# A decoder block on one core: the attention's projections, turns and softmaxes in another order, the rotation on another engine

## The chip, the cores and the metric

The kernel runs on one core of a Trainium2 chip. A core has a tensor engine (PE; its weight loads are listed apart as PEld), a vector engine (DVE), a scalar engine (ACT), GpSimd (POOL) and a queue that only issues transfers (SP). PE writes its products to eight banks of PSUM; the other data lies in SBUF. The metric is the time of one execution in microseconds. Three runs of the kernel before gave 361.92, 362.18 and 362.21, median 362.18. One execution was profiled; its trace is what the numbers below come from.

## The reference

One decoder layer on 256 tokens of width 1024. Two attention branches of eight heads with 64 columns each run side by side: MoBA, whose q and k are normalized and rotated (with 256 tokens it is plain causal attention), and FoX, whose scores get a bias from a cumulated forget gate. Two sigmoid gates merge them, and a gated feed-forward part follows.

```python
h = rms_norm(x, attn_norm_g)
proj = h @ w_in
qa, ka, va, qb, kb, vb, f_logit, g_logit = split(proj)
qa = partial_rope(rms_norm(split_heads(qa)), pos)      # the first 16 columns of each head
ka = partial_rope(rms_norm(split_heads(ka)), pos)
o_a = merge_heads(moba_attention(qa, ka, va))
qb, kb = rms_norm(split_heads(qb)), rms_norm(split_heads(kb))
o_b = merge_heads(forgetting_attention(qb, kb, vb, log_sigmoid(f_logit + b_forget)))
gates = sigmoid(g_logit + b_gate)
x = x + (gates[0] * (o_a @ w_branch_moba) + gates[1] * (o_b @ w_branch_fox)) @ w_out
up = rms_norm(x, ffn_norm_g) @ w_ffn_up
u, g = split(up)
x = x + (silu(causal_depthwise_conv(g)) * u) @ w_ffn_down
```

## The kernel before

**Products.** Every matrix product is made of three: each float32 operand is split into a high part (ACT copies it, `whi`, line 136) and the rest (DVE subtracts, `wlo`, line 137), and PE adds high x high, high x low and low x high. A weight comes by a transfer of 1 MB into `raw` (three buffers), and is split in two units of 1024 columns; `whi` and `wlo` have six buffers each, and `use` asks for units five ahead. A unit's split can only start when PE has read the buffer that it gets. These 120 pairs of splits run through the whole program beside whatever else DVE and ACT do.

**Stages.** `project_qk` computes q and k of MoBA from the first loads (banks `pq`, `pk`). `project` computes one of the other q, k, v in 48 products of 512 columns (line 291), `twin` one 256-column pair of a weight in 48 products of 256 columns (lines 513 to 515); `gate(c)` is such a pair for both merge gates, read out of its bank by DVE (line 522). `finish_qk` normalizes q or k per head: ACT squares the bank (305), DVE sums (306), a chain of small operations gives the factor (219 to 223, 309), DVE multiplies the bank by it (315), and for MoBA rotates 16 columns of each head (322 to 325). `turn_qk` transposes the result on PE (341, 64 columns each) and ACT copies it to `qT`, `kT` (346). `scores` multiplies q and k (434) into six banks; `softmax` adds mask or bias (450), takes exponentials on ACT (453) and scales (458), a pair of heads at a time. `turn` transposes the probabilities (469, 48 transposes in six banks, copied out by ACT at 473), `values` multiplies them with v (485), and ACT and DVE split the result into `oh`, `ol` (499, 500). The forget gate is a small product (362), summed by another (372), then a chain on a few rows (378 to 399) that ends with a transfer through DRAM and `forget_bias` (408 to 414).

**Order.** PE runs in the order in which the code is written. For DVE, ACT and POOL a scheduler sets the order at build time by priority; `soon()` raises what is inside it by 45 places of the program. Each engine then runs its list strictly in order. A bank is handed on when its last reader is done, so a product that starts a bank can wait for DVE or ACT.

The code at the end (lines 536 to 594) writes the attention as: MoBA's q, k; v; FoX's q; forget gate; turn of MoBA's q, k; FoX's k with the scores of MoBA in its middle; FoX's v; gate 0; turn of FoX's q, k and of MoBA's probabilities; gate 1; MoBA's values and FoX's scores; gates 2 to 6; turn of FoX's probabilities; gate 7; FoX's values. Behind that come the branch projection, the output projection and the feed-forward part, which the change leaves alone.

Of the kernel before, what the change touches and what calls it, by code (L numbers as in the profile page):

```python
# [32 lines left out]
SOON = 45  # L33
# [11 lines left out]
def decoder_block(ctx, tc, a, out):  # L45
# [36 lines left out]
    chunks = [("qkv", m, h) for m in range(4) for h in range(2)]  # L82
    chunks += [("wg", c) for c in range(KT)]
# [18 lines left out]
    def load(upto):  # L102
        while state["next"] <= min(upto, len(units) - 1):
# [30 lines left out]
            for j in range(n):  # L134
                s = slice(j * w, (j + 1) * w)
                i = nc.scalar.activation(hi[:, s], raw[:, s], AF.Copy)  # L136
                d = nc.vector.tensor_tensor(lo[:, s], raw[:, s], hi[:, s].bitcast(F32), op=ALU.subtract)  # L137
                if (c, h) == (("qkv", 0, 1), 0):
                    after(i, rs_done[0])
                    after(d, rs_done[1])  # L140
                if (c, h) == (("qkv", 0, 0), 0):
                    first_lo.append(d)
                if c[0] == "head" and j == 0:
                    after(d, xlo)
# [91 lines left out]
    def norm1_sums():  # L236
        nc.scalar.activation(flat[:, 0], xss[:, 1], AF.Copy)
        low = nc.gpsimd.tensor_tensor(flat[:, 1], xss[:, 1], flat[:, 0].bitcast(F32), op=ALU.subtract)
        for i in casts:
            after(i, low)  # L240
        ssp = bank()[:, 0:S]
# [56 lines left out]

    def finish_qk(br, pts):
# [11 lines left out]
        for m, (isk, pt) in enumerate(pts):  # L311
            qn = T([P, NT, NH, HD], "qn", 2)
            qns.append(qn)
            for t in range(NT):
                nc.vector.tensor_tensor(qn[:, t], pt[t].rearrange("p (h d) -> p h d", h=NH),
                                        f[:, m, t, :, None].to_broadcast([P, NH, HD]), op=ALU.mult)
            if br == 0:
                rc, rsn = rope[isk]
                p1 = T([P, NT, NH, 16], "p1", 1)
                p2 = T([P, NT, NH, 16], "p2", 1)  # L320
                x16 = qn[:, :, :, 0:16]
                nc.vector.tensor_tensor(p1, x16, rc[:, :, None, :].to_broadcast([P, NT, NH, 16]), op=ALU.mult)
                nc.vector.tensor_tensor(p2, x16, rsn[:, :, None, :].to_broadcast([P, NT, NH, 16]), op=ALU.mult)
                nc.vector.tensor_tensor(qn[:, :, :, 0:8], p1[:, :, :, 0:8], p2[:, :, :, 8:16], op=ALU.add)
                nc.vector.tensor_tensor(qn[:, :, :, 8:16], p1[:, :, :, 8:16], p2[:, :, :, 0:8], op=ALU.add)
# [3 lines left out]
    qT = T16(4, "qT", F32)  # L329
    kT = T16(4, "kT", F32)  # L330
    halves = (slice(0, HD), slice(HD, P))

    def turn_qk(qn, br, isk):
# [8 lines left out]
        dst = (kT if isk else qT).rearrange("p b (m c) -> p m b c", m=4)  # L342
# [23 lines left out]
    def row(i):  # L366
        return gates[:NH, i // 2, i % 2]
# [49 lines left out]
    oh = T16(KT, "oh")  # L417
    ol = T16(KT, "ol")
    probs = {}
    last_exp = []  # L420

    def scores(br):
# [5 lines left out]
        for n, pair in enumerate(range(4)):  # L428
            for t in range(NT):
                for c, q in enumerate(QUARTERS[t]):  # L430
                    seen = slice(0, (q + 1) * HD) if t == 0 else slice((3 - q) * HD, S)
                    keys = slice(seen.start + (1 - t) * P, seen.stop + (1 - t) * P)
                    for j, r in enumerate(halves):
                        nc.tensor.matmul(piece(n, t, j)[halves[c], seen], qT[r, pair, q * HD:(q + 1) * HD], kT[r, pair, keys], start=True, stop=True)  # L434
# [7 lines left out]
    def softmax(br, pair, sps):  # L442
        s = T([P, 2, 384], "s", 4)
        nm = T([P, 2, 2], "nm", 4)
        l = T([P, 2, 2], "l", 4)
        for j in range(2):
            h = 2 * pair + j
            sp = sps[j]
            for i, c in enumerate((slice(0, 128), slice(128, 384))):
                nc.vector.tensor_tensor_reduce(s[:, j, c], sp[i], mask3[:, c] if br == 0 else bias[:, h, c],  # L450
                                               scale=1.0, scalar=3e38, op0=ALU.add, op1=ALU.min, accum_out=nm[:, j, i:i + 1])
            for i, c in enumerate((slice(0, 128), slice(128, 384))):
# [9 lines left out]
    def turn(br):  # L462
        pT = T([P, 4, 2, 384], "pT")
# [7 lines left out]
        for i in range(3):  # L471
            for h in range(2):
                nc.scalar.activation(dst[:, h, 8 * i:8 * i + 8], tps[i][h].rearrange("p (g c) -> p g c", g=8), AF.Copy)
        for pair in range(4):
            probs[br, pair] = pT[:, pair]

    def values(br):
        ops = banks()
        o4 = [o.rearrange("p (h b t) -> p h b t", h=2, b=4) for o in ops]

        def product(o, r, k, b, c, pair, j, start, stop):
# [6 lines left out]
        for i, k, b, c in ((0, 0, 0, two), (1, 0, 2, both), (1, 1, 1, two)):  # L488
            for pair in range(4):
                for j, m in enumerate(halves):  # L490
                    product(o4[i][m, c, pair], full, k, b, c, pair, j, b != 1 and pair == 0, False)
        for pair in range(4):
            for j, m in enumerate(halves):
                product(o4[0][m, 0, pair], halves[0], 0, 0, one, pair, j, False, pair == 3)
                product(o4[1][m, 0, pair], halves[1], 1, 1, one, pair, j, False, pair == 3)
        b = slice(4 * br, 4 * br + 4)
        for i in range(2):
            h, l = (v[:, b, i * P:(i + 1) * P].rearrange("p b (h t) -> p h b t", h=2) for v in (oh, ol))
            copied = nc.scalar.activation(h, o4[i], AF.Copy)
            nc.vector.tensor_tensor(l, o4[i], h.bitcast(F32), op=ALU.subtract)  # L500
        return copied
# [17 lines left out]
    def gate(c):  # L519
        gp = bank()  # L520
        twin("wg", c, gp, xh, xl)
        return nc.vector.tensor_tensor(gates[:, c], gp.rearrange("p (b t) -> p b t", b=2), rsB[:, None, :].to_broadcast([P, 2, S]), op=ALU.mult)
# [7 lines left out]
    def soon():  # L530
        return tc.high_priority(offset=SOON)

# [3 lines left out]
    pq, pk, pv = banks(), banks(), banks()  # L536
# [8 lines left out]
    with soon():  # L545
        qn, kn = finish_qk(0, ((0, pq), (1, pk)))
# [3 lines left out]
    pq, pk = banks(), banks()  # L550
    project(3, pq, 0)
    project(3, pq, 1)
    with soon():
        forget_a()
    turn_qk(qn, 0, 0)
    turn_qk(kn, 0, 1)
    with soon():
        qn, = finish_qk(1, ((0, pq),))
    def between():
        with soon():  # L560
            forget_b()
    project(4, pk, 0, between)
    with soon():
        sps = scores(0)
        for pair in range(2):
            done = softmax(0, pair, sps[pair])
    forget_chain(done)
    project(4, pk, 1)
    with soon():
        kn, = finish_qk(1, ((1, pk),))  # L570
    for pair in range(2, 4):
        done = softmax(0, pair, sps[pair])
# [4 lines left out]
    first = gate(0)  # L577
    with soon():
        forget_bias(first)
    turn_qk(qn, 1, 0)  # L580
    turn_qk(kn, 1, 1)
    turn(0)
    gate(1)
    values(0)
    for pair, sp in enumerate(scores(1)):
        softmax(1, pair, sp)
    gate(2)
    gate(3)
    gate(4)
    gate(5)  # L590
    gate(6)
    turn(1)
    gate(7)
    copied = values(1)
# [206 lines left out]
```

## Time and profile before

| | us |
|---|---|
| median of three runs | 362.18 |
| profiled execution, time | 361.99 |
| its span in the trace | 360.2 |
| PE busy | 355.0 |
| DVE busy | 276.0 |
| ACT busy | 217.9 |
| POOL busy | 26.3 |

The mean granted clock of PE was 0.999. The attention that the change touches lies between 27 and 132 us of the span. Rows of the trace give a start, a duration, the engine, the line, the operation and what is written from what; rows of groups give the busy time and the mean of one in ns, then the idle time ahead of it and what ended that.

### The profile page before, as it was taken

The numbers are of one execution on the slowest core, as the hardware profiler recorded it, in microseconds if no ns is written. First come the engines' busy times: TensorE is split into PE (matmuls) and PEld (weight loads), VectorE is DVE, ScalarE is ACT, GpSimd is POOL, SyncE is SP. The second block draws the span as 40 slices with busy tenths as digits, with TensorE's granted clock in tenths as the row PEclk, the third lists the DMA queues.
The fourth block names the chain that finished last, engine by engine and source line by source line (L and its number), as shares of the span: only waits on it lengthen the run. The fifth ranks groups of instructions, "written<-read, shape, count | busy, mean of one in ns | idle before, by whom it ended". The sixth has DMA issues, their size and how long they took to land.

```text
span 360.2 us, 7565 instructions
## 1 busy us (share of the span) xinstructions
PE 355.0 (99%) x3119; PEld 337.2 (94%) x3119; DVE 276.0 (77%) x491; ACT 217.9 (60%) x363; POOL 26.3 (7%) x43
## 2 busy tenths in 40 slices
PE   9999999999999999999999999999999999999995
PEld 4788878899999999999999999999999999999994
DVE  5899698999897547875979776868677777768643
ACT  5859666988598765545876654655554554555420
POOL 2542002200000000000530000000000000000000
PEclk9999999999999999999999999999999999999999
DMA  7986665174606644455364565464565464563003
GB/s 275 402 318 244 238 229 186 56 285 186 235 3 250 231 172 152 152 216 212 140 235 173 179 235 173 179 235 162 191 231 168 185 233 149 204 225 128 0 2 116
DMA packets 12130, 68.28 MB, mean 190 GB/s; under 512 B 1688, under 2 KB 2848, under 8 KB 4672
## 3 DMA queue, kind: packets, MB, share of 16 engines
q1 hardware_dynamic: 11664, 66.62, 51.1%
q0 software_dynamic: 288, 1.19, 0.9%
q8 instruction: 24, 0.39, 0.4%
q14 instruction: 10, 0.08, 0.1%
q10 hardware_dynamic: 144, 0.00, 0.0%
HBM read 66.75 MB, written 1.06 MB: 188 GB/s over the span
## 4 chain that ended last, share of the span: by engine, by line
PE 99%; DVE 0%; issue 0%
PE bank L513 15%; PE bank L515 15%; PE bank L514 15%; PE bank L291 12%; PE bank L277 6%; PE bank L715 6%; PE bank L713 6%; PE bank L714 6%; PE bank L611 2%; PE bank L637 2%; PE bank L613 2%; PE bank L612 2%; PE bank L639 2%; PE bank L638 2%; PE bank L485 1%; PE bank L434 1%
## 5 line engine op out<-in xcount | busy, mean ns | idle before, releaser
L137 DVE TENSOR_TENSOR wlo<-raw,whi 128x1024 fp32r<-128x1024 f32 x120 | 146.8, 1227 | 51.5 <-ACT whi L136 51.4
L136 ACT ACTIVATE whi<-raw 128x1024 fp32r<-128x1024 f32 x120 | 126.4, 1058 | 74.8 <-PE bank L514 44.1
L515 PE MATMUL bank<-oh,wlo 128*128 128x256 f32 x352 | 96.8, 275 | 0.0
L513 PE MATMUL bank<-oh,whi 128*128 128x256 f32 x352 | 96.8, 275 | 0.0
L514 PE MATMUL bank<-ol,whi 128*128 128x256 f32 x352 | 96.8, 275 | 0.0
L513 PEld LDWEIGHTS bank<-oh,whi 128*128 128x128 f32 x352 | 66.1, 188 | 0.0
L514 PEld LDWEIGHTS bank<-ol,whi 128*128 128x128 f32 x352 | 66.1, 188 | 0.0
L515 PEld LDWEIGHTS bank<-oh,wlo 128*128 128x128 f32 x352 | 66.1, 188 | 0.0
L513 PE MATMUL bank<-xh,whi 128*128 128x256 f32 x128 | 35.6, 278 | 0.0
L515 PE MATMUL bank<-xh,wlo 128*128 128x256 f32 x128 | 35.3, 275 | 0.0
L514 PE MATMUL bank<-xl,whi 128*128 128x256 f32 x128 | 35.2, 275 | 0.0
L513 PEld LDWEIGHTS bank<-xh,whi 128*128 128x128 f32 x128 | 24.0, 188 | 0.5 <-DVE ol L500 0.3
L514 PEld LDWEIGHTS bank<-xl,whi 128*128 128x128 f32 x128 | 24.0, 188 | 0.0
L515 PEld LDWEIGHTS bank<-xh,wlo 128*128 128x128 f32 x128 | 24.0, 188 | 0.0
L291 PE MATMUL bank<-whi,xh 128*128 128x512 f32 x64 | 21.2, 392 | 0.0
L291 PE MATMUL bank<-whi,xl 128*128 128x512 f32 x64 | 21.0, 389 | 0.0
L291 PE MATMUL bank<-wlo,xh 128*128 128x512 f32 x64 | 21.0, 388 | 0.0
L680 DVE TENSOR_TENSOR sq<-bank,rs 128x512 f32<-128x512 f32 x22 | 15.1, 691 | 6.6 <-PE bank L515 6.5
L611 PE MATMUL bank<-oh,whi 128*128 128x256 f32 x64 | 17.7, 277 | 0.0
L613 PE MATMUL bank<-oh,wlo 128*128 128x256 f32 x64 | 17.6, 275 | 0.0
L612 PE MATMUL bank<-ol,whi 128*128 128x256 f32 x64 | 17.6, 275 | 0.0
L637 PE MATMUL bank<-xh,whi 128*128 128x256 f32 x64 | 17.6, 275 | 0.0
(179 smaller groups left out, 743.1 us busy)
## 6 DMA issues: line engine op xcount, KB each, us to landing
raw<-in_wu SPq DMA_DIRECT2D x22, 1024.0 KB, 4.8
raw<-in_wd SPq DMA_DIRECT2D x11, 1024.0 KB, 4.8
raw<-in_qkv SPq DMA_DIRECT2D x8, 1024.0 KB, 5.2
raw<-in_wg SPq DMA_DIRECT2D x8, 1024.0 KB, 5.0
raw<-in_wb SPq DMA_DIRECT2D x4, 1024.0 KB, 4.8
raw<-in_wo SPq DMA_DIRECT2D x4, 1024.0 KB, 4.8
raw<-in_head SPq DMA_DIRECT2D x6, 512.0 KB, 6.6
gates<-cd POOLq DMA_DIRECT2D x1, 1024.0 KB, 5.0
```

Of the source, the lines that this page charges most:

```text
L136: i = nc.scalar.activation(hi[:, s], raw[:, s], AF.Copy)
L137: d = nc.vector.tensor_tensor(lo[:, s], raw[:, s], hi[:, s].bitcast(F32), op=ALU.subtract)
L277: nc.tensor.matmul(pt[t], lhs[:, k, t * P:(t + 1) * P], rhs, start=(k == 0 and i == 0), stop=(k == KT - 1 and i == 2))
L291: nc.tensor.matmul(pt[t], lhs[:, k, t * P:(t + 1) * P], rhs[:, c], start=(k == 0 and i == 0), stop=(k == KT - 1 and i == 2))
L513: nc.tensor.matmul(o, wh[:, w], mh[:, k], start=(k == 0 and i == 0), stop=False)
L514: nc.tensor.matmul(o, wh[:, w], ml[:, k], start=False, stop=False)
L515: nc.tensor.matmul(o, wl[:, w], mh[:, k], start=False, stop=(k == KT - 1 and i == 1))
L611: nc.tensor.matmul(o, wh[:, w], oh[:, 4 * br + k], start=(k == 0), stop=False)
L612: nc.tensor.matmul(o, wh[:, w], ol[:, 4 * br + k], start=False, stop=False)
L613: nc.tensor.matmul(o, wl[:, w], oh[:, 4 * br + k], start=False, stop=(k == 3))
L637: nc.tensor.matmul(o, wh[:, w], mh[:, k], start=(k == 0 and i == 0), stop=False)
L713: nc.tensor.matmul(o, wh[:, w], ah, start=(p == 0 and h == 0 and c == 0), stop=False)
```

## The change

- The projections stand in another order: MoBA's q, k, then FoX's q, k (their normalization raised by 160 places), gate 0, then all four turns with the forget gate's product ahead of the last, gate 1, MoBA's scores, MoBA's v, gate 2, FoX's scores, FoX's v, gates 3 to 5, both turns of probabilities, gate 6, both values, gate 7. The list of loads follows.
- The rotation's four operations per tile go from DVE to GpSimd.
- Each gate's read out of its bank is raised by 160 places, and the softmaxes are ordered behind such a read.
- FoX's normalized q, k, their turned copies, its softmax and its turned probabilities live in the buffers of `ol`, `oh`, `qn` and `bias`, since both branches are now alive at once.
- The sigmoids of the gates are ordered behind the copies of FoX's turned probabilities, in place of its last exponential.
- The sum of the first normalization uses the bank of the warm-up.

```diff
-    chunks = [("qkv", m, h) for m in range(4) for h in range(2)]
-    chunks += [("wg", c) for c in range(KT)]
+    chunks = []
+    for m in (1, 2, "wg0", "wg1", 0, "wg2", 3, "wg3", "wg4", "wg5", "wg6", "wg7"):
+        chunks += [("wg", int(m[2:]))] if isinstance(m, str) else [("qkv", m, h) for h in range(2)]
...
+            if br == 0:
+                qn = T([P, NT, NH, HD], "qn", 2)
+            else:
+                qn = qn1[:, 4 * isk:4 * isk + 4].rearrange(...)
...
-                nc.vector.tensor_tensor(p1, x16, rc[:, :, None, :].to_broadcast([P, NT, NH, 16]), op=ALU.mult)
+                nc.gpsimd.tensor_tensor(p1, x16, rc[:, :, None, :].to_broadcast([P, NT, NH, 16]), op=ALU.mult)
...
-    def values(br):
-        ops = banks()
+    def values():
+        oh, ol = T16(KT, "oh"), T16(KT, "ol")
+        ops = [banks() for br in range(2)]
...
     def gate(c, between=None):
...
+        with soon(FIRST):
+            return nc.vector.tensor_tensor(gates[:, c], gp.rearrange("p (b t) -> p b t", b=2), rsB[:, None, :].to_broadcast([P, 2, S]), op=ALU.mult)
...
+    for isk in range(2):
+        pt = banks()
+        project(3 + isk, pt, 0)
+        project(3 + isk, pt, 1)
+        with soon(FIRST):
+            qkn += finish_qk(1, ((isk, pt),))
+    gate(0)
+    with soon():
+        for i, qn in enumerate(qkn):
+            if i == 3:
+                forget_a()
+            turn_qk(qn, i // 2, i % 2)
...
+    read = gate(1, between)
+    with soon():
+        for pair, sp in enumerate(scores(0)):
+            scaled = softmax(0, pair, sp, read)
...
+    read = gate(2)
+    with soon():
+        forget_bias(read)
+    with soon():
+        for pair, sp in enumerate(scores(1)):
+            softmax(1, pair, sp, read)
...
+    with soon():
+        turn(0)
+        last_exp[:] = [turn(1)]
     gate(6)
+    oh, ol, copied = values()
     gate(7)
```

In the changed kernel the lines are shifted: the split stands at 137 and 138, squares at 308, sums at 309, normalization at 321, transposes of q and k at 348, the forget gate's product at 369, transposes of probabilities at 483, their copies at 487, a gate's products at 531 to 533 and its read at 541.

PE, around the forget gate's product and the turns of q and k; first before (the turn of MoBA's q, k, in the middle of FoX's projections):

```order
L291 MATMUL bank<-whi,xl 128x512 x2
L291 MATMUL bank<-wlo,xh 128x512 x2
L362 MATMUL bank<-xT,wfg 32x256 x8
L341 MATMUL bank<-cst,qn 128x64 x32
L291 MATMUL bank<-whi,xh 128x512
L291 MATMUL bank<-whi,xl 128x512
L291 MATMUL bank<-wlo,xh 128x512
```

and now, between gate 0 and gate 1 (`qn` are MoBA's q and k, `ol` holds FoX's):

```order
L532 MATMUL bank<-xl,whi 128x256
L533 MATMUL bank<-xh,wlo 128x256
L348 MATMUL bank<-cst,qn 128x64 x32
L348 MATMUL bank<-cst,ol 128x64 x16
L369 MATMUL bank<-xT,wfg 32x256 x8
L348 MATMUL bank<-cst,ol 128x64 x16
L531 MATMUL bank<-xh,whi 128x256
L532 MATMUL bank<-xl,whi 128x256
```

All four turns are one piece behind gate 0; FoX's q comes third, its k last. The bank of q's second half is the one that gate 0 had, and k's tile must be normalized by DVE.

DVE, at the normalization of a FoX tile; before (FoX's q):

```order
L306 TENSOR_REDUCE ss<-sq 128x8 x2
L137 TENSOR_TENSOR wlo<-raw,whi 128x1024
L219 TENSOR_SCALAR qfv<-ss 128x16
L221 SCALAR_TENSOR_TENSOR qfv<-qfv 128x16
L222 TENSOR_TENSOR qfv<-qfv 128x16
L223 SCALAR_TENSOR_TENSOR qf<-qfv 128x16
L309 TENSOR_TENSOR qf<-qf,rsw 128x16
L315 TENSOR_TENSOR qn<-bank,qf 128x512 x2
```

and now (FoX's k, with the read of gate 0 at L541):

```order
L309 TENSOR_REDUCE ss<-sq 128x8 x2
L138 TENSOR_TENSOR wlo<-raw,whi 128x1024
L220 TENSOR_SCALAR qfv<-ss 128x16
L138 TENSOR_TENSOR wlo<-raw,whi 128x1024
L222 SCALAR_TENSOR_TENSOR qfv<-qfv 128x16
L138 TENSOR_TENSOR wlo<-raw,whi 128x1024
L223 TENSOR_TENSOR qfv<-qfv 128x16
L541 TENSOR_TENSOR gates<-bank,rsB 128x512
L224 SCALAR_TENSOR_TENSOR qf<-qfv 128x16
L138 TENSOR_TENSOR wlo<-raw,whi 128x1024
L312 TENSOR_TENSOR qf<-qf,rsw 128x16
L321 TENSOR_TENSOR ol<-bank,qf 128x512 x2
```

Four splits and the read of gate 0 stand between the sums and the normalization, where one split stood.

ACT, at the copies of the turned probabilities; before (FoX's, the second turn):

```order
L526 ACTIVATE gates<-gates,sm 128x256 x2
L136 ACTIVATE whi<-raw 128x1024 x2
L526 ACTIVATE gates<-gates,sm 128x256
L473 ACTIVATE pT<-bank 128x8x64 x6
L526 ACTIVATE gates<-gates,sm 128x256
L136 ACTIVATE whi<-raw 128x1024 x2
```

and now (`pT` MoBA's, `bias` FoX's, L545 the gates' sigmoids):

```order
L137 ACTIVATE whi<-raw 128x1024 x6
L487 ACTIVATE pT<-bank 128x8x64 x6
L487 ACTIVATE bias<-bank 128x8x64 x6
L545 ACT_TABLE_LOAD
L545 ACTIVATE gates<-gates,sm 128x256 x2
L137 ACTIVATE whi<-raw 128x1024
```

Twelve copies follow each other behind six splits; the load of the sigmoid's table, which came ahead of the second turn, is behind them.

More of the change, by code (lines that the diff above doesn't have):

```diff
@@ L366, in row @@
     def row(i):
-        return gates[:NH, i // 2, i % 2]
+        return gates[:NH, 4 + i // 2, i % 2]
     def forget_b():
@@ L440, in scores, with softmax @@
         return [[[piece(n, t, j) for t in range(NT)] for j in range(2)] for n in range(4)]
-    def softmax(br, pair, sps):
-        s = T([P, 2, 384], "s", 4)
+    def softmax(br, pair, sps, done):
+        if br == 0:
+            s = T([P, 2, 384], "s", 4)
+        else:
+            if not homes:
+                two = T([P, KT * S + 64], "ol")
+                homes.extend(two[:, i * 768:(i + 1) * 768] for i in range(2))
+                homes.extend(T([P, 1024], "qn", 2)[:, 0:768] for i in range(2))
+            s = homes[pair].rearrange("p (j c) -> p j c", j=2)
         nm = T([P, 2, 2], "nm", 4)
@@ L487, in values @@
         one, two, both, full = slice(0, 1), slice(1, 2), slice(0, 2), slice(0, P)
-        for i, k, b, c in ((0, 0, 0, two), (1, 0, 2, both), (1, 1, 1, two)):
+        for br, o4 in enumerate(o4s):
+            for i, k, b, c in ((0, 0, 0, two), (1, 0, 2, both), (1, 1, 1, two)):
+                for pair in range(4):
+                    for j, m in enumerate(halves):
+                        product(o4[i][m, c, pair], full, k, b, c, br, pair, j, b != 1 and pair == 0, False)
+        for br, o4 in enumerate(o4s):
             for pair in range(4):
                 for j, m in enumerate(halves):
[L491 to L501, printed above, removed]
+                    product(o4[0][m, 0, pair], halves[0], 0, 0, one, br, pair, j, False, pair == 3)
+                    product(o4[1][m, 0, pair], halves[1], 1, 1, one, br, pair, j, False, pair == 3)
+            b = slice(4 * br, 4 * br + 4)
+            for i in range(2):
+                h, l = (v[:, b, i * P:(i + 1) * P].rearrange("p b (h t) -> p h b t", h=2) for v in (oh, ol))
+                copied = nc.scalar.activation(h, o4[i], AF.Copy)
+                nc.vector.tensor_tensor(l, o4[i], h.bitcast(F32), op=ALU.subtract)
+        return oh, ol, copied
     def twin(kind, c, dst, mh, ml, late=False, between=None):
@@ L517, in twin, with gate @@
                     between()
[L519 removed]
+    def gate(c, between=None):
         gp = bank()
[L521 to L522 removed]
+        twin("wg", c, gp, xh, xl, between=between)
+        with soon(FIRST):
+            return nc.vector.tensor_tensor(gates[:, c], gp.rearrange("p (b t) -> p b t", b=2), rsB[:, None, :].to_broadcast([P, 2, S]), op=ALU.mult)
     def gate_sigmoid(c):
@@ L576, in decoder_block @@
     finish_v(pv, 1)
[L577 to L587, printed above, removed]
     gate(3)
```

78 lines of the change are left out of this document (32 added, 46 removed).

## The prediction

> **What bounds the kernel now.** I read the page first: its busy shares, the idle times of the tensor engine, then the chain that ended last.
>
> ```profile
> span 360.2 us, 7565 instructions
> PE 355.0 (99%) x3119; PEld 337.2 (94%) x3119; DVE 276.0 (77%) x491; ACT 217.9 (60%) x363; POOL 26.3 (7%) x43
> PEclk9999999999999999999999999999999999999999
> PE 99%; DVE 0%; issue 0%
> ```
>
> The span is a string of matrix products at full granted clock; no other engine has a share in the chain. A busy PE could still hide short waits, so I asked who PE waited for:
>
> ```profile
> PE bank L190 <- PEq L794: 0.8, 1, 0.8
> ```
>
> That is the whole answer: 0.8 us at the start, nothing later. So the change cannot take away a wait, since there is none. It can only save what PE spends on going into and out of its stretches of small products, and it can add waits. The chain, in order of time, prices the stretches (start, us, line, count):
>
> ```profile
> 27.40 21.76 PE bank L291 x96
> 49.16 1.00 PE bank L362 x16
> 50.16 1.14 PE bank L341 x32
> 51.30 2.93 PE bank L291 x12
> ...
> 54.46 2.74 PE bank L291 x12
> 57.20 2.33 PE bank L434 x46
> ...
> 76.11 0.12 PE bank L513
> ...
> 81.55 1.15 PE bank L341 x30
> 82.70 1.75 PE bank L469 x48
> 84.45 0.32 PE bank L513
> 84.76 0.12 PE bank L514
> ...
> 90.14 2.58 PE bank L485 x80
> 92.72 2.18 PE bank L434 x46
> ...
> 122.35 1.65 PE bank L469 x44
> ...
> 129.67 2.58 PE bank L485 x80
> ```
>
> A twin of 48 products takes 81.55 - 76.11 = 5.44 us (gate 0). The first product behind a stretch takes 0.32 in place of 0.12 (84.45 against 84.76), or 12 take 2.93 in place of 2.74: 0.2 us for each return.
>
> **Term 1, the stretches.** Before, small products come in six groups: forget gate and first turn, scores 0, second turn and probabilities 0, values 0 and scores 1, probabilities 1, values 1. After, five: all turns with the forget gate, scores 0, scores 1, both probabilities, both values. One return less: -0.2. The values of both branches enter their form once, not twice: some -0.1 by the same price. Scores 1 now stand alone, as scores 0 do (2.33 against 2.18 behind the values): +0.15. The forget gate lies between transposes, one more change of form: up to +0.2. Both probabilities together: some -0.15. I take -0.3, with bounds -0.6 and 0. All other products are the same ones, so nothing larger than 0.6 us can be won by this change on PE.
>
> **Term 2, the turn of FoX's k.** Here the new order puts PE right behind DVE. Times as in the trace of before as long as PE does the same: q's and k's FoX projections are 96 products of L291's kind, 27.40 to 49.16, gate 0 runs to 54.60. Then PE transposes q, k (MoBA), q (FoX), multiplies the forget gate, transposes k (FoX). Without waits that takes 1.00 + 1.14 + 1.15 + 0.2, some 3.5 us, and the last eight transposes (second half of the rows) start near 57.6. What must be ready is k's finish: two squares on ACT, then the DVE rows shown in the section on the change. Their prices stand in the groups of the trace from 20 to 136 us and in DVE's timeline:
>
> ```profile
> L305 ACT ACTIVATE sq<-bank,rsw 128x512 f32<-128x512 f32 x8 | 5.1, 676 | 0.0
> L522 DVE TENSOR_TENSOR gates<-bank,rsB 128x512 f32<-128x512 f32 x8 | 5.4, 678 | 0.9 <-PE bank L515 0.9
> ...
> 49.92 1.22 DVE L137 TENSOR_TENSOR wlo<-raw,whi 128x1024 fp32r<-128x1024 f32 x1
> 51.06 0.41 DVE L364 TENSOR_TENSOR aT<-bank,aT 128x256 fp32r<-128x256 f32 x1
> 51.39 1.27 DVE L306 TENSOR_REDUCE ss<-sq 128x8 f32<-128x512 f32 x2
> ...
> 54.62 0.17 DVE L222 TENSOR_TENSOR qfv<-qfv 128x16 f32<-128x16 f32 x1
> 55.31 1.29 DVE L315 TENSOR_TENSOR qn<-bank,qf 128x512 f32<-128x512 f32 x2
> 56.52 0.40 DVE L373 TENSOR_TENSOR gates<-bank,rsB 8x256 f32<-8x256 f32 x1
> ```
>
> A split steps on by 1.14 (51.06 - 49.92), a pair of reduces by 1.2, a pair of normalizations takes 1.29, a small operation 0.1 beside others and 0.2 in a dependent chain. ACT has one split (1.06) ahead of k's squares, whose buffer a product near 48.7 gives free; the two squares of 0.68 end at 50.4 and 51.0, the second reduce at 51.6. Behind it stand three splits and three small rows: 3 x 1.14 + 0.3, so gate 0's read starts at about 55.3, though its products end at 54.60: DVE is 0.6 to 0.7 late. That read stands ahead of k's last factors by its raised priority. From its start to the end of the second normalization: 0.6 (read, in steps) + 0.1 + 1.14 (a split) + 0.2 + 1.29 = 3.3, hence 58.6. PE, ready for it at 57.6, waits about 1.1 us in sum; the first part of it already at q's transposes, whose bank is the one that gate 0's read gives free.
>
> The rotation, now on GpSimd, runs beside this: q's MoBA tile is normalized near 47, k's near 49, and each then takes two operations of 128x256 and two of half that. By GpSimd's rows below, 0.8 us for 128x256 and 0.5 as an estimate for the half, 2.6 for a tile, k's ends at about 52, over two microseconds ahead of the first transpose at 54.6, so both are hidden; if GpSimd took twice as long on these strided shapes, k's turn would come 1 us late. DVE is rid of these eight operations, which the 55.3 above already leaves out. But GpSimd's work is not free for DVE:
>
> ```profile
> 18.87 1.76 DVE L137 TENSOR_TENSOR wlo<-raw,whi 128x1024 fp32r<-128x1024 f32 x1
> ...
> 21.50 1.21 DVE L137 TENSOR_TENSOR wlo<-raw,whi 128x1024 fp32r<-128x1024 f32 x1
> ...
> 13.80 5.74 POOL L183 TENSOR_TENSOR xss<-xss,sq 128x256 f32<-128x256 f32 x5 [4.18 <-ACT sq L179]
> 20.44 0.79 POOL L183 TENSOR_TENSOR xss<-xss,sq 128x256 f32<-128x256 f32 x1 [0.89 <-ACT sq L179]
> ```
>
> While GpSimd adds (13.80 to 19.54), a split took 1.76 us, against 1.21 at 21.50. Two splits lie beside the rotation; 0 to 2 x 0.55 = 1.1 us more. One of them has 0.4 of idle time behind it (the wait for the squares), so I take +0.35. Term 2: +1.45, bounds 0.35 (DVE in time: the 3.3 from 54.6 ends at 57.9) and 2.2.
>
> [...]
>
> **Term 3, both probabilities in one stretch.** 96 transposes need 12 banks and there are eight. So turn 1's third and fourth pair wait until ACT has copied turn 0's first ones out.
>
> ```profile
> 122.33 1.06 ACT L136 ACTIVATE whi<-raw 128x1024 fp32r<-128x1024 f32 x1 [1.67 <-PE bank L514]
> 123.30 0.49 ACT L526 ACTIVATE gates<-gates,sm 128x256 f32<-128x256 f32 x1
> 123.70 3.01 ACT L473 ACTIVATE pT<-bank 128x512 f32<-128x512 f32 x6
> ```
>
> There a split starts on ACT with the stretch (122.33, the stretch 122.35), the next operation 0.95 later, and the copies follow every 0.5 (3.01 for six). In the new order, too, a split that waits for the last product ahead of the stretch (gate 5's) stands before the copies. So copy n ends 1.1 + 0.5 n behind the stretch's start, the fourth, on which turn 1's last pair of banks depends, at 3.1. PE would be there at 1.65 + 2/3 x 1.65 = 2.75 and waits 0.35, more by a hand-over or two: 0.4. Before, the second turn had 0.1 of this kind (1.75 against 1.65 for the same transposes). Net +0.3, bounds 0 and 0.7.
>
> **What else moves, at nothing.** The MoBA softmax and its own splits run on DVE while PE computes v and gate 2 (16.3 us); FoX's bias and softmax beside v and gates 3 to 5 (27 us). DVE's busy share and the softmax's rows say that there is little room:
>
> ```profile
> 60.00:80.00 20.00, 20.00 (x107) 17.20 (x107) 19.62 (x80) 16.98 (x46) 4.38 (x9) 1.00 0.44 163
> ...
> L458 DVE TENSOR_SCALAR s<-s,r 128x256 f32<-128x256 f32 x16 | 5.4, 340 | 0.0
> L458 DVE TENSOR_SCALAR s<-s,r 128x128 f32<-128x128 f32 x16 | 4.4, 274 | 0.0
> L450 DVE CUSTOM_DVE_ANT_0 s<-bank,cst 128x256 f32<-128x256 f32 x8 | 3.2, 405 | 0.0
> L450 DVE CUSTOM_DVE_ANT_0 s<-bank,cst 128x128 f32<-128x128 f32 x8 | 2.2, 273 | 0.0
> ```
>
> (The window gives PE, PEld, DVE, ACT, POOL busy in 20 us, the clock, the DMA share.) A branch's softmax is 3.2 + 2.2 + (5.4 + 4.4)/2 = 10.3 us on DVE. Behind gate 1's read, which ends near 66, stand that, seven splits (8.0) and 2 us of small rows, so gate 2's read ends near 86.5. The bank that it frees is wanted by FoX v's second half: 66 + scores 2.5 + v 10.9 + gate 2 5.4 + scores 2.5 + six products 1.4, near 88. The cover is 1.5 to 2 us, and FoX's first scores leave their banks about as long before gate 3 wants one; beyond it a slip of DVE costs PE its own length. The sixteen sigmoids now precede the values' copies on ACT, beside gates 6 and 7; the copies still end over 1 us before the branch projection reads them. The loads come in another order, but the DMA engines are 0.44 busy in that window, and no wait of PE names one.
>
> **The sum.** The profiled execution before took 361.99 (span 360.2), 0.19 below the median of 362.18. 361.99 - 0.3 + 1.45 + 0.3 = 363.4 us.
>
> **Rivals.**
> - *DVE keeps up.* If the DVE rows up to gate 0's read are over by 54.6, only 0.35 of term 2 is left: 361.99 - 0.3 + 0.35 + 0.3 = 362.3; without term 3, 362.0. For it: DVE is rid of eight operations, and 0.6 us is within the error of such a sum of thirty rows. Against it: the late rows hang on ACT's squares, which cannot start before 49.16 and a split that ends at 49.7. It decides at a backlog of 0.6 us, some half of a split.
> - *GpSimd holds DVE longer.* Both splits are held for a whole operation, 2 x 0.79 by the row at 20.44, in place of the 0.35 in the sum: 363.4 + 1.2 = 364.6; the same if the softmax outruns its cover by 1 us. It decides where a split has no idle time behind it. Against it: no split in the trace was held for more than 0.55. [...]
> - *Faster.* The mechanism is the change of form on PE: if DVE and ACT are in time and the groups cost more than the returns show (0.6 saved), the time is 361.4. It needs both waits gone and the far bound of term 1.
> - *The change does not do what it says:* the order shows that it does; its scores stay apart in two stretches.
>
> **How the numbers follow.** Forecast (both waits, 362.9 to 364.2): 0.53. DVE keeps up (361.6 to 362.9): 0.29. Held longer (364.2 to 365.0, some beyond): 0.14. Faster: 0.04. A measurement of this kernel tells 0.2%, 0.72 us, from no change; so slower means above 362.9: 0.53 + 0.14 = 0.67; faster, below 361.45: 0.04; the rest, 0.29, is within. The range 361.7 to 365.0 leaves out the faster case and the end of the slow one.
>
> **What would show it.** PE's waits name DVE at the turns near 56 to 59 (by 1 to 2 us) and ACT at the probabilities near 116; the chain has a share of DVE; the values' 80 and both probabilities' 96 transposes appear as one piece each; a split beside the rotation lasts over 1.3 us. If PE names nobody there, terms 2 and 3 are wrong and the time is 361.7. If it names a bank at gate 3 or at v's second half, the cover that I counted was too thin.

## The result, and the profile after

| | before | after |
|---|---|---|
| median of six runs each | 362.14 | 366.14 |
| all runs | 361.92 to 362.46 | 364.58, 364.91, 365.97, 366.32, 366.58, 366.58 |
| profiled execution, its span | 361.99, 360.2 | 364.58, 362.8 |
| PE's small-product stretches, in sum | 16.38 | 19.93 |

The changed kernel is slower: the ratio is 1.0102, with a 95% interval of 1.0079 to 1.0124. Its executions fall into two groups, 364.6 to 364.9 at a mean granted clock of 0.999 to 1.0, and 366.0 to 366.6 at 0.994 to 0.995; the profiled one is the fastest. Forecast was 363.4, range 361.7 to 365.0.

The page after the change: the span, the busy times, the clock by slices, and the chain that ended last by engine.

```profile
span 362.8 us, 7564 instructions
PE 354.6 (98%) x3119; PEld 337.7 (93%) x3119; DVE 274.4 (76%) x483; ACT 218.0 (60%) x363; POOL 34.2 (9%) x51
PEclk9999999999999999999999999999999999999999
PE 94%; DVE 2%; DMA 1%; issue 1%; ACT 1%; DVEq 0%
```

DVE has lost only 1.6 us of busy time, though the rotation's 2.8 came off it; and the chain, which was 99% PE, now passes through DVE, DMA and ACT. The view of PE's waits (engine, line, waited for, us in total, times, longest) says where:

```profile
PE bank L483 <- DVE gates L541: 1.9, 1, 1.9
PE bank L191 <- PEq L812: 0.8, 1, 0.8
PE bank L348 <- DVE gates L541: 0.7, 1, 0.7
PE bank L348 <- DVE ol L321: 0.4, 1, 0.4
PE bank L278 <- ACT whi L137: 0.2, 1, 0.2
```

Two places: the turns (L348) and the probabilities (L483). PE's timeline shows both (start, us, line, count, and in brackets the idle time named):

```profile
54.17 1.21 PE L348 MATMUL bank<-cst,qn 64*128 64x64 f32 x32
55.22 0.22 PE L348 MATMUL bank<-cst,ol 64*128 64x64 f32 x1
56.17 0.71 PE L348 MATMUL bank<-cst,ol 64*128 64x64 f32 x15 [0.72 <-DVE gates L541]
...
58.29 0.97 PE L348 MATMUL bank<-cst,ol 64*128 64x64 f32 x16 [0.41 <-DVE ol L321]
59.19 0.38 PE L531 MATMUL bank<-xh,whi 128*128 128x256 f32 x1
...
113.73 1.72 PE L483 MATMUL bank<-cst,s 64*128 64x64 f32 x48
115.29 0.22 PE L483 MATMUL bank<-cst,ol 64*128 64x64 f32 x1
117.44 0.96 PE L483 MATMUL bank<-cst,ol 64*128 64x64 f32 x23 [1.92 <-DVE gates L541]
...
119.11 0.39 PE L531 MATMUL bank<-xh,whi 128*128 128x256 f32 x1
```

From its first small product to the first large one behind it the stretch of the turns takes 59.19 - 54.17 = 5.02 us, that of the probabilities 119.11 - 113.73 = 5.38. A kernel of the experiments below in which PE waits at neither place (all edits and the copies) shows what the same products take without a wait, 57.91 - 54.62 = 3.29 and 116.05 - 112.54 = 3.51:

```profile
54.62 1.21 PE L360 MATMUL bank<-cst,qn 64*128 64x64 f32 x32
...
57.91 0.39 PE L543 MATMUL bank<-xh,whi 128*128 128x256 f32 x1
...
112.54 1.72 PE L495 MATMUL bank<-cst,s 64*128 64x64 f32 x48
...
116.05 0.39 PE L543 MATMUL bank<-xh,whi 128*128 128x256 f32 x1
```

So the **turns lose 1.73, the probabilities 1.87**. Without waits the five stretches of the new order sum to 16.34 against 16.38 for the six of before, and there is one return less (0.2): -0.24. Together +3.36; the profiled executions differ by 2.59. Of the other 0.77, 0.37 lies in small gaps of PE in the first 12 us, which differ by 0.45 between two profiled executions of the changed kernel too, and 0.34 behind PE's last product; the rest is not traced.

What PE waited for is read on DVE. Its timeline at both places:

```profile
52.38 0.43 DVE L220 TENSOR_SCALAR qfv<-ss 128x16 f32<-128x16 f32 x1
52.73 1.21 DVE L138 TENSOR_TENSOR wlo<-raw,whi 128x1024 fp32r<-128x1024 f32 x1
53.86 0.42 DVE L222 SCALAR_TENSOR_TENSOR qfv<-qfv 128x16 f32<-128x16 f32 x1
54.21 1.21 DVE L138 TENSOR_TENSOR wlo<-raw,whi 128x1024 fp32r<-128x1024 f32 x1
...
55.43 0.68 DVE L541 TENSOR_TENSOR gates<-bank,rsB 128x512 f32<-128x512 f32 x1
...
57.45 1.29 DVE L321 TENSOR_TENSOR ol<-bank,qf 128x512 f32<-128x512 f32 x2
...
106.57 0.66 DVE L541 TENSOR_TENSOR gates<-bank,rsB 128x512 f32<-128x512 f32 x1
107.15 1.00 DVE L472 TENSOR_SCALAR qn<-qn,r 128x128 f32<-128x128 f32 x4
108.06 4.62 DVE L138 TENSOR_TENSOR wlo<-raw,whi 128x1024 fp32r<-128x1024 f32 x4
...
115.56 1.23 DVE L138 TENSOR_TENSOR wlo<-raw,whi 128x1024 fp32r<-128x1024 f32 x1 [1.14 <-ACT whi L137]
116.70 0.68 DVE L541 TENSOR_TENSOR gates<-bank,rsB 128x512 f32<-128x512 f32 x1
```

At the turns, gate 0's products end at 54.2, but its read starts at 55.43, behind the three splits that follow k's sums (51.24, 52.73, 54.21). At the probabilities gate 5's read starts at 116.70, three microseconds after its products, behind a split that itself waited for ACT. That split is of the first branch weight, the load that ACT waited for (timelines of SP and of ACT):

```profile
109.34 9.53 SPq L130 DMA_DIRECT2D raw<-in_wb  x4
```

```profile
114.46 2.00 ACT L137 ACTIVATE whi<-raw 128x1024 fp32r<-128x1024 f32 x2 [4.22 <-PE bank L483]
116.37 3.02 ACT L487 ACTIVATE pT<-bank 128x512 f32<-128x512 f32 x6
```

The bracket names PE for ACT's 4.22 us, but the split starts 0.38 after the load has landed (114.08). In two runs below the same load lands at 114.60 and at 113.21, and this split starts 0.38 later each time (114.98, 113.59): it is the load that it waits for. The load was issued at 109.34, when the first of the four splits at 108.06 had freed a `raw` buffer. So there were two theories to test: the wait at the turns is DVE's backlog of splits, and the wait at the probabilities is gate 5's read behind a split whose load is late. The two groups of times were a third thing to explain.

### The profile page after: what moved, and what is told of

It reads as the page before. It is cut to its first block, busy times and chain, and to the rows that moved or that the text cites. A ratio compares the mean times of both kernels' runs of the same rounds, so it can differ in the third digit from the quotient of the medians.

```text
span 362.8 us, 7564 instructions
## 1 busy us (share of the span) xinstructions
PE 354.6 (98%) x3119; PEld 337.7 (93%) x3119; DVE 274.4 (76%) x483; ACT 218.0 (60%) x363; POOL 34.2 (9%) x51
## 3 DMA queue, kind: packets, MB, share of 16 engines
HBM read 66.75 MB, written 1.06 MB: 187 GB/s over the span
## 4 chain that ended last, share of the span: by engine, by line
PE 94%; DVE 2%; DMA 1%; issue 1%; ACT 1%; DVEq 0%
PE bank L531 15%; PE bank L533 15%; PE bank L532 14%; PE bank L292 12%; PE bank L278 6%; PE bank L733 6%; PE bank L732 5%; PE bank L731 5%; PE bank L657 2%; PE bank L631 2%; PE bank L656 2%; PE bank L655 2%; PE bank L630 2%; PE bank L629 2%; PE bank L501 1%; PE bank L440 1%
```

## The experiments

Each kernel is the changed one with the edit shown, unless said otherwise; "wait" is a stretch's length beyond 3.29 (turns) or 3.51 (probabilities), 1.73 and 1.87 in the changed kernel. The expectations give the second as the whole gap from 115.29 to 117.44, 2.15, which is 0.28 more, and the first as 1.67. Medians stand against that of the kernel before in the same session, 361.8 to 361.9.

### The changed kernel again

> The changed kernel again, unchanged, beside the others on one chip. Theory (its idle stretch of 2.15 us makes the granted clock fall in some executions): two or more of the executions at 0.994 to 0.995 and 365.9 to 366.7, the others at 0.998 or more and 364.5 to 365.0. Rival (that spread belonged to one chip or one hour): all within 0.5 us.

364.62 once, 366.51 to 366.80 four times (clock 0.995). The spread belongs to the kernel. The profiled execution is one of the four; it is read under the granted clock.

### The probabilities: order, load, both

Order: the first branch weight's split is put behind gate 5's read.

```diff
+                if (c, h) == (("wb", 0), 0):
+                    after(d, state["read"])
...
+        cap = pos[("wg", 7), 1] if c == ("wg", 5) else len(units)
+        load(... min(pos[c, h] + AHEAD, cap))
...
-    gate(5)
+    state["read"] = gate(5)
```

> The split of the first branch weight is put behind gate 5's read on VectorE, and its load one unit later; PE's order stays. Theory (the hole at the probabilities is that read, standing behind a split whose load came late): the wait of 2.15 us near 115 goes, and with it 1.9 to 2.2 us of the profiled execution's 364.58, hence 362.4 to 362.7; the wait at the turns near 55 to 58.5 (1.67 in sum) stays. Rival A (VectorE is simply behind with its work there, or ScalarE's copies of the first branch's probabilities would be next): a wait of 0.5 or more stays at the probabilities or at the branch projection, 363.1 or more. On the clock: if the hole at the probabilities makes the granted clock fall in some executions, all are at 0.998 or more and within 0.5 us of each other; if the hole at the turns does, some still show 0.994 and 1.4 to 2 us more.

Median 364.54, 1.0086 [1.0068, 1.0104]. **The theory fell as put**: the wait stayed as long (1.87), only its name changed. PE's waits, then ACT's timeline:

```profile
PE bank L486 <- ACT pT L490: 1.5, 3, 1.1
```

```profile
114.98 2.01 ACT L137 ACTIVATE whi<-raw 128x1024 fp32r<-128x1024 f32 x2 [3.66 <-PE bank L486]
116.90 3.02 ACT L490 ACTIVATE pT<-bank 128x512 f32<-128x512 f32 x6
```

ACT, too, runs its list in order, and in it the same late split stands ahead of the copies that free the banks. The edit did not delay the load: it landed 0.34 behind the start of the stretch, as in the changed kernel (0.35). The load had held two engines; DVE was only the one that came last.

Load: the weight goes into the two buffers of MoBA's q and k, long free, so that it waits for no split.

```diff
+                    if c == ("wb", 0):
+                        state["home"] = [T([P, 1088], tag)[:, 4:1028] for tag in ("qT", "kT")]
+                        for i in range(2):
+                            loads[c] = nc.sync.dma_start(state["home"][i], src[:, i * 1024:(i + 1) * 1024])
...
```

> The first branch weight is loaded into the two buffers that held q and k of the first branch, which are free long before, so its load waits for no split; the split still stands ahead of gate 5's read. Theory (about half of the hole is the load that waited for a buffer, the rest is the split itself ahead of the read): the wait near 115 shrinks from 2.15 to 0.9 to 1.1, the profile to 363.4 to 363.7. Rival (the load alone): it goes wholly, 362.4 to 362.7. Rival (the load is no part of it): it stays at 2.0 or more.

Median 363.57, 1.0044 [1.0032, 1.0056]; the wait falls to 4.05 - 3.51 = 0.54 (0.82 as a gap, 0.9 to 1.1 expected; the profiled time of 363.01 is 0.4 below the expectation), and no execution is below a clock of 0.999. What is left is DVE's order (its timeline):

```profile
113.01 1.22 DVE L143 TENSOR_TENSOR wlo<-raw,whi 128x1024 fp32r<-128x1024 f32 x1
114.14 1.22 DVE L143 TENSOR_TENSOR wlo<-qT,whi 128x1024 fp32r<-128x1024 f32 x1
115.28 0.69 DVE L546 TENSOR_TENSOR gates<-bank,rsB 128x512 f32<-128x512 f32 x1
```

Both edits together:

> Both edits together: the first branch weight is loaded early into the first branch's q and k buffers, and its split on VectorE stands behind gate 5's read. In the two single edits the wait of 2.15 at the probabilities was 2.2 with the order alone (the same late load then held ScalarE's split and with it its copies) and 0.85 with the early load alone (VectorE's split of 1.14 still ahead of the read). Theory now (one late load held both engines; behind it VectorE's order is worth 0.85): the wait is 0 to 0.4, what is left being ScalarE's copies, the profile 362.1 to 362.6, every execution at a clock of 0.998 or more. Rival (the copies of the first branch's probabilities are the next limit by themselves): a wait of 0.6 or more on ScalarE stays, 362.8 or more.

Median 362.86, 1.0025 [1.0013, 1.0036]; PE's wait there is now one of 0.2 for ACT's copies, and the profiled time of 362.92 missed the expectation by 0.3; it lies where the rival put it (362.8 or more), but the rival's wait of 0.6 on ACT did not come. The stretch is at 3.74: the load first (1.87 to 0.54), the order behind it (0.54 to 0.23). The amended theory holds for the wait.

### Why the load was late: the raised priorities

Only the gates' reads go back from 160 to 45.

```diff
-        with soon(FIRST):
+        with soon():
             return nc.vector.tensor_tensor(gates[:, c], ...
```

> Only the gates' reads go back from 160 to 45; FoX's finish keeps its 160. In VectorE's order one row moves: the split that frees the buffer for the first branch weight's load stands ahead of FoX's last normalization and gate 3's read, not behind them. Theory (that raised read passed this split, and the load's lateness at the probabilities comes from there): the split ends 1.5 us earlier, the load is issued 1.5 earlier relative to the stretch, the wait at the turns stays at 1.67 and the one at the probabilities falls from 2.15 to about 1.0, where VectorE's own two splits ahead of gate 5's read are the limit; all executions at 0.997 or more and at 363.2 to 363.9. Rival (the load is late for another reason, and what shortened the wait with both priorities undone was that PE came later): the wait stays at 1.8 or more, and some executions at 0.995.

Median 363.62, 1.005 [1.0036, 1.0064]: **one row of DVE's order is worth 2.5 us of the median**, the clock of the slower executions included. Gate 3's read and one split change places in DVE's list; nothing else in it differs, and the lists of ACT and GpSimd are the same. DVE's timeline, then the load's issue from SP's:

```profile
107.14 1.20 DVE L138 TENSOR_TENSOR wlo<-raw,whi 128x1024 fp32r<-128x1024 f32 x1
108.25 1.01 DVE L472 TENSOR_SCALAR qn<-qn,r 128x128 f32<-128x128 f32 x4
109.17 0.69 DVE L541 TENSOR_TENSOR gates<-bank,rsB 128x512 f32<-128x512 f32 x1
```

```profile
108.40 9.82 SPq L130 DMA_DIRECT2D raw<-in_wb  x4
```

The split at 107.14 stood behind the read and the softmax's last step before (106.57, 107.15, then 108.06); now the load is issued 5.9 us ahead of the stretch's start (108.40 against 114.32) in place of 4.4 (109.34 against 113.73). The wait falls from 1.87 to 4.11 - 3.51 = 0.60, and no execution is below 0.998.

Both uses of 160 undone, that of FoX's finish too:

> The changed kernel with the raised priority of the gates' reads and of FoX's finish undone (160 back to 45). VectorE's order then puts FoX q's normalization behind two more splits, gate 0's read ahead of one split instead of behind it, and gate 3's and 4's reads later by a split. Theory (the raised priority is not the cause; both waits are splits and one late load that it does not move): the waits at the turns and at the probabilities each stay within 0.6 of 1.67 and 2.15, the lowest time 364.2 to 365.4, some executions at a clock of 0.995. Rival (the priority made the backlog): one of the two waits falls by 1 or more, lowest time below 363.7. Rival (the priority saved time): a wait grows by 1 or more, lowest time above 365.6.

Median 364.13, 1.0056 [1.0043, 1.007], no execution below 0.997. The wait at the probabilities falls as above (DVE named with 0.7); that at the turns grows by half a microsecond (1.0 and 0.6 named, in place of 0.7 and 0.4). This is the first rival's result in the main, though its bound of 363.7 was missed by 0.1: the raised reads cost more than they bring, FoX's raised finish helps.

### The turns: splits, rotation

Four splits of v's weights are put behind k's normalization; the rotation stays on GpSimd.

```diff
+                if c in (("qkv", 0, 0), ("qkv", 0, 1)):
+                    after(d, state["norm"])
...
...
+        cap = pos[("wg", 1), 1] if c[:2] == ("qkv", 2) else len(units)
...
```

> Only the splits are moved: four splits of v's weights that stood on VectorE ahead of or between gate 0's read and k's normalization are put behind both; the rotation stays on GpSimd. Theory (the wait at the turns is VectorE's backlog of splits, 1.67 us, and GpSimd's part in it small): the normalization is done by 54, the read ends at 55.3, the wait at the turns falls to 0 to 0.3 and the wait at the probabilities stays at 2.15, the profile at 362.9 to 363.3. Rival (GpSimd holds VectorE's operations beside it): a wait of 0.7 or more stays at the turns, 363.6 or more. Rival (the four splits come late for v): a new wait of PE near 68.

The turns take 58.05 - 54.77 = 3.28: the wait is gone, PE names only the probabilities (2.0). Executions of 362.91 and 363.59 (the profiled one, 0.3 above the expectation) beside three of 364.2 at 0.995; median 364.2, 1.0054 [1.004, 1.0067]. The normalization did not end by 54 but at 55.8, since its factor waited 1.33 for ACT; PE needed it no earlier. No new wait came at v.

The rotation's four lines back to DVE (`nc.gpsimd` to `nc.vector`):

> The rotation back on VectorE (eight operations of 2.8 us in sum by the profile before). Three of the four splits that stood ahead of gate 0's read then stand behind k's normalization (3.6 us), so the read can start when gate 0's last product has ended. Theory (the wait at the turns is the backlog of VectorE ahead of that read, splits included): it falls from 1.67 to 0 to 0.4 us, the profile to 363.1 to 363.4; the wait of 2.15 at the probabilities stays. Rival (the rotation on GpSimd relieves VectorE, and its 2.8 us come on top): the wait at the turns grows to 3 or more, 366 or more. Rival (GpSimd holds VectorE): no stretch of VectorE between 48 and 56 us differs by more than 0.5 us from the sum of its rows, and the gain is that alone, 364.1.

Median 363.96, 1.0068 [1.0051, 1.0085]; the wait at the turns falls to 3.85 - 3.29 = 0.56, more than the 0.4 that I allowed, though DVE does 2.8 us more: three splits have moved behind the normalization. Order, not load, decided here too.

The kernel **before**, with only its rotation moved to GpSimd:

> The kernel before with only its rotation moved to GpSimd. Theory (where the two meet, GpSimd is held and VectorE hardly): VectorE's splits beside it stay at 1.21 to 1.25, a GpSimd operation of 0.46 to 0.74 lasts up to 1.5, k's rotation ends near 51 and its turn waits 0 to 0.6; the median within -0.1 and +0.6 of the kernel before. Rival (VectorE is held, as where a split took 1.76 beside GpSimd's sums): two splits at 1.6 or more and a later read of gate 0, +0.5 to +1.2. Rival (relief of VectorE pays): -0.3 or less.

Median 364.52, 1.0072 [1.0047, 1.0098]: worse than I expected on any theory. PE's waits, then the timelines of GpSimd and of DVE:

```profile
PE bank L341 <- POOL qn L325: 2.0, 1, 2.0
```

```profile
47.31 1.60 POOL L322 TENSOR_TENSOR p<-qn,rc 128x256 f32<-128x256 f32 x1
48.87 1.72 POOL L323 TENSOR_TENSOR p<-qn,rsn 128x256 f32<-128x256 f32 x1
50.66 1.32 POOL L324 TENSOR_TENSOR qn<-p,p 128x128 f32<-128x128 f32 x1
51.94 0.45 POOL L325 TENSOR_TENSOR qn<-p,p 128x128 f32<-128x128 f32 x1
```

```profile
44.00 7.67 DVE L137 TENSOR_TENSOR wlo<-raw,whi 128x1024 fp32r<-128x1024 f32 x5
```

Beside no split the same operations took 0.74 (at 42.97) and 0.45 (at 51.94) in this run; here they step by 1.3 to 1.8, and five splits take 7.67 instead of 5 x 1.14 + 0.08 = 5.8. Both engines take longer, and k's tile ends at 52.4, two microseconds after PE wanted it. In the changed kernel the turns come later (54.17, and GpSimd ends at 54.26), so that the rotation is just hidden there.

### All edits together, and the copies

Early load, order at gate 5's read and late splits of v:

> The early load, the order at gate 5's read and the late splits of v together. Theory (the two waits are all that the change lost; what is left is what it gains in the tensor engine's stretches): both waits at 0.4 or less in sum 0.6, the profile 360.9 to 361.6, a ratio to the kernel before of 0.997 to 0.999. Rival (a further backlog of VectorE, with four splits moved back, opens a third wait): 362 or more. Rival (the stretches gain nothing): 361.8 to 362.2.

Median 361.46, 0.9988 [0.998, 0.9997]: no wait at the turns (57.97 - 54.68 = 3.29), 0.2 named at the probabilities, all executions at 0.998 or more; the profiled one, 361.74, is 0.1 above the expectation. The two waits, with the clock that they cost, were all that was lost; what remains is a gain of about a tenth of a per cent.

And with the second half of the branch weight's split behind the copies on ACT:

```diff
+                if (c, h) == (("wb", 0), 1):
+                    after(i, state["copied"])
...
```

> The kernel with all three edits and one more: on ScalarE, the second half of the first branch weight's split stands behind the copies of the first branch's probabilities. Theory (term 3: the second branch's banks wait for copies that stand behind a split): the wait of 0.21 that the profile names there, and up to 0.25 that it spreads, go; the stretch of both probabilities falls from 3.95 to 3.5 to 3.75 beyond its large products, the median from 361.46 to 361.0 to 361.3. Rival (the transposes of 96 need their time anyway, or the bank's read is next): within 0.1 of 361.46.

Median 361.45, 0.9982 [0.9974, 0.9991]. PE's stretch of probabilities falls by 0.23, and the view of waits names nobody but PE's own start.

The median did not follow (361.45 against 361.46, in two sessions); both kernels are faster than the one before by 0.1 to 0.2%.

### The granted clock

Nine products of constants into the first bank of FoX's turn, which is free; it is the second that PE waits for. So PE is busy in the wait (10.00 of the 10 us from 115, 8.08 in the changed kernel), and the transposes overwrite the products:

```diff
+        for j in range(9 * br):
+            nc.tensor.matmul(tps[0][0], warm[:, 0:P], warm, start=True, stop=True)
```

> Nine products of 128x512 of constants are added into the first bank of the second branch's probabilities, ahead of its transposes, which overwrite it: work that is no part of the reference's computation, put where PE waits for 2.15 us, so that PE is busy in the wait and the wait itself is as long. Theory (two groups of times of the changed kernel, 364.6 to 364.9 and 366.0 to 366.6, are the granted clock falling after PE's idle stretch of 2.15 us): all executions are at a clock of 0.998 or more and 364.4 to 365.1, the median falls from 366.1 to about 364.7. Rival (the wait at the turns, or something that has nothing to do with idle PE, moves the clock): both groups stay, median 365.5 to 366.6.

Five executions from 364.53 to 364.93, all at 0.999 or more, median 364.63: with nothing saved and work added (the transposes behind the wait go on 3.72 us after the start of the stretch, 3.71 in the changed kernel), the median is 1.5 to 1.9 below that of the changed kernel. The profile of the changed kernel again, an execution at 0.995, shows the fall itself. Windows of 1 us; PE busy comes second, the granted clock behind the five engines:

```profile
117.00:118.00 1.00, 0.06 (x2) 0.06 (x3) 1.00 (x3) 1.00 (x3) 0.00 (x0) 1.00 0.95 401
118.00:119.00 1.00, 1.00 (x28) 1.00 (x30) 1.00 (x1) 1.00 (x3) 0.00 (x0) 0.82 1.03 434
119.00:120.00 1.00, 1.00 (x24) 1.00 (x21) 0.01 (x1) 1.00 (x3) 0.00 (x0) 0.50 0.20 74
120.00:121.00 1.00, 1.00 (x8) 0.88 (x5) 0.00 (x0) 1.00 (x3) 0.00 (x0) 0.50 0.84 147
121.00:122.00 1.00, 1.00 (x7) 1.00 (x6) 0.00 (x0) 1.00 (x3) 0.00 (x0) 0.50 1.04 426
122.00:123.00 1.00, 1.00 (x10) 1.00 (x9) 0.00 (x0) 0.98 (x3) 0.00 (x0) 0.97 1.08 434
```

The clock falls to half some 0.7 us after PE has gone on (117.94), and stays there for about 3.4: (0.18 + 3 x 0.50 + 0.03) = 1.7 us lost, which is about the distance of the two groups (1.4 to 2.2). Two more profiles are of executions at 0.995, with the rotation on DVE and with the split done three times (below): there the fall comes 1.9 and 1.7 us after PE has gone on, and the half clock lasts as long.

To see whether the wait alone does it, I took the kernel with all three edits and repeated one split ahead of gate 5's read, twice more and once more (the same values):

```diff
+                if (c, h) == (("wg", 7), 1):
+                    for _ in range(2):
+                        d = nc.vector.tensor_tensor(lo[:, s], raw[:, s], hi[:, s].bitcast(F32), op=ALU.subtract)
+                    state["again"] = d
...
```

> The kernel with all three edits, and the split ahead of gate 5's read done three times instead of once (the same values again): 2.28 us more on VectorE, nothing else moved. Theory (the wait at the probabilities alone makes the granted clock fall, whatever its cause): PE waits there 1.7 to 2.1 us, the best executions take 363.0 to 363.6 at 0.998 or more, and some of the executions 1.5 to 2.0 us more at 0.994 to 0.996. Rival (what moved the clock was the late load or both waits together): the wait comes, and all executions are within 0.6 us of each other at 0.998 or more.

Median 363.68, 1.005 [1.0038, 1.0061]; a wait of 2.0, and two of six executions at 0.994 and 0.995. They took 364.3, some 0.6 to 1.2 more than the others, less than the 1.5 expected. The profiled one of the two lost 1.7 to the half clock like the changed kernel, so its other parts must have been shorter: its first 12 us were, by 0.67, against the profile of the three edits. Whether that is all is open.

> As the run with the split done three times, but done twice: 1.14 us more on VectorE ahead of gate 5's read. Theory (a wait below about 1.1 us costs its own length and leaves the clock alone, one of 1.7 or more makes it fall in about half of the executions): a wait of 0.6 to 1.0 at the probabilities, every execution at 0.997 or more, 362.0 to 362.9. Rival (the chance of a fall grows in proportion to the wait): one or two of six executions at 0.995.

Eleven executions, none below 0.999, a wait of 0.8, median 361.81 (below the 362.0 to 362.9 expected), 1.0 [0.9991, 1.0009]. Over all kernels, by the longest wait that PE's view of waits names behind its start:

| longest wait | kernels | executions | of them at 0.995 or less |
|---|---|---|---|
| 1.7 to 2.0 us | changed; late splits; rotation on DVE; before with GpSimd; split three times | 34 | 18 |
| 1.1 | order alone | 6 | 1 |
| 1.0 or less | the eight others | 60 | 0 |

The last row does not count the kernel before, which has no such wait and was never below 0.997. In the row of 1.1 PE loses 1.87 at the same place, but in three pieces. The long wait lies at the turns in one kernel of the first row (before with GpSimd) and at the probabilities in the others, so the place does not decide.

## Why the prediction was wrong, point by point

- **Bound.** Right: nothing on PE to win but the stretches. *Term 1* (-0.3) measures -0.24, from the kernel without waits; its own items add up to -0.3 only without the forget gate's +0.2, to -0.1 with it.
- **Term 2**, the turn of FoX's k, was right in mechanism and nearly in size: 1.73 against 1.45. The read came at 55.4 (predicted 55.3), the normalization ended at 58.7 (predicted 58.6). Moving the splits took the whole wait away, so it was their backlog; GpSimd's share on DVE was small and not where the term had it: two small operations took 0.43 and 0.42 in place of 0.17, the splits took 1.21 to 1.25. The rotation itself, which was to end near 52 and over two microseconds early, ended at 54.26, since three of GpSimd's operations took 1.52 to 1.61 in place of 0.46 and 0.74; PE's turns start at 54.17 with q's tile and name no wait for it.
- **Term 3**, the copies behind a split, exists with 0.23 where nothing else is late (0.3 predicted). The wait of 1.87 at the same place is not it.
- **The step that failed** is "What else moves, at nothing", in two sentences. "The loads come in another order, but the DMA engines are 0.44 busy in that window, and no wait of PE names one": a share of busy time says nothing of when a load can be issued. The load waited for a buffer, the buffer for a split, the split for a read that the change had raised past it (1.27 of the 1.87 by the run that lowers the reads, 1.33 by the early load; of the rest, 0.31 goes with DVE's order and 0.23 is term 3). And FoX's softmax "beside v and gates 3 to 5 (27 us)" was weighed as a sum, and the order in which reads, splits and softmax stand in it was not followed to its end; gate 5's read was not in the working at all. By the profiled execution the sum was 1.2 too low: 1.87 in place of 0.3, plus 0.3 more at the turns, less 0.7 at both ends of the span, which no term had.
- **The clock** was no term and no rival: a wait of 2 us was priced at its length. In eight of eleven executions it cost another 1.4 to 2.2, which is what put the median out of the range. With the predicted waits (1.45 in two parts, and 0.3) the table above gives hardly a fall; so this error follows from the one before.
- **Rivals.** DVE did not keep up. "GpSimd holds DVE longer" names 364.6, which the profiled execution met by accident: the splits beside the rotation took 1.21 to 1.25. That a split is held for a whole operation of GpSimd, as its 1.2 supposes, no run shows; most was lost with the rotation alone moved, 1.9 over five splits (7.59 from start to start in place of 5 x 1.14). (The row of 1.76 behind the 0.35 of term 2 was thinner than it looked, too: in the trace before, the split at 16.71 beside the same sums took 1.35, so what a split loses there varies.) The far side, a gain, appears only when the waits are removed by other means.

## What to carry to other kernels

A priority raised for one operation passes everything between, and what it passes may be the release of a buffer on which a load waits: follow each passed row to what it frees, not only the raised row to what it feeds (one such row was worth 2.5 us of the median here). Where an in-order queue holds a row that waits for a load, look at every engine that has such a row; removing it from one shows the next (the wait of 1.87 stayed 1.87 here). And price a wait of PE of 2 us by its length plus the clock that it may cost (1.7 us in each of three profiles here).

## What the runs showed of the hardware

In three profiles (the changed kernel again, the rotation on DVE, the split done three times) the granted clock fell to 0.50 for about 3.4 us, 0.7 to 1.9 us after PE had gone on from a single wait of 1.7 to 2.0 us; each lost 1.7 us by it. These three executions have a mean clock of 0.995. So low a mean came in 18 of 34 executions of the kernels whose profile names such a wait, and in none of 60 of those whose profile names waits of at most 1.0. Why it came in about half of the 34 and not in the others was not shown.

The rotation's operations on GpSimd took longer beside DVE's splits. In the changed kernel three of the eight took 1.52, 1.52 and 1.61, each starting 0.01 to 0.26 us behind the start of a split (48.60, 51.24, 52.73); the other five, which start beside DVE's normalizations and sums, took 0.46 to 0.76. The splits there took 1.21 to 1.25; in the kernel before with the rotation moved five splits stepped by 1.52 on average in place of 1.14. Two rows of GpSimd's timeline after the change, the same operation on q's and on k's tile:

```profile
48.32 0.46 POOL L331 TENSOR_TENSOR qn<-p,p 128x128 f32<-128x128 f32 x1
...
52.74 1.52 POOL L331 TENSOR_TENSOR qn<-p,p 128x128 f32<-128x128 f32 x1
```

The difference, 1.06, is nearly the step of a split (1.14), and a split starts at 52.73, just ahead of the second row; the first starts beside a pair of normalizations (47.41). By what means the two engines slow each other was not shown.
